# One sum of weights per pair moved from VectorE to an accumulating DMA, and a plain filler in the first pair of each chain, in a Mamba-2 layer in fp32

## The chip, the cores and the metric

The kernel runs on one core of a Trainium2 chip. The time is the device time of one execution in microseconds (us). TensorE (PE) multiplies, VectorE (DVE) and ScalarE (ACT) do the elementwise work, SyncE (SP) issues most transfers, and GpSimd (POOL) issues those that add to their destination.

## The reference, cut to what matters

DEPTH is 1, so the layer is the Mamba-2 mixer alone: 512 tokens, 2048 features, inner width 4096, 64 heads of 64 in 8 groups, a state of 128.

```python
def reference(x, ln_g, final_g, ssm_w_in, ...):
    hn = rmsnorm(x, ln_g[0])
    x = x + ssm_mixer(hn, ...)
    return rmsnorm(x, final_g)

def ssm_mixer(h, w_in, conv_w, conv_b, dt_bias, a_log, d_skip, norm_g, w_out):
    proj = h @ w_in                       # 2048 -> z 4096, x 4096, B 1024, C 1024, dt 64
    xbc = silu(causal_depthwise_conv(xbc, conv_w, conv_b))
    dt = softplus(dt + dt_bias)
    a = -exp(a_log)
    y = ssd_chunked_scan(xs * dt[..., None], dt * a, bm, cm)
    y = y + d_skip * xs
    y = rmsnorm(y * silu(z), norm_g)
    return y @ w_out                      # 4096 -> 2048
```

All is float32.

## The kernel before

**Products in three parts.** A float32 product is made of three matmuls on rounded halves: weights are split into `hi` (ACT rounds, L87) and `lo` (DVE subtracts, L88), the input into `xh` and `xl`, and PE adds hi times xh, hi times xl and lo times xh. So each 512 KB piece of weights costs one load, one cast on ACT and one subtraction on DVE before PE can use it. The halves of a piece lie in one of three `hi`/`lo` buffers; some pieces have buffers of their own (`h1h`/`h1l` for R11, `oh`/`ol` in the output projection).

**Plain tiles and pairs.** The input projection has 80 tiles of 128 columns. The first eight (`plain`: B0, C0, x0, z0, x1, z1, B1, C1) are computed directly, 16 k-steps of six 256-column matmuls each (`mm_k`). The other 72 go in 36 pairs (`quads`), one pair being two tiles, by a scheme of Strassen's kind: the two tiles times the two halves of the inner dimension make four blocks of weights R11, R12, R21, R22, and seven products replace eight. Each product (`product`) is 4 steps of six matmuls, and a pair is 28 steps (`QS`). The blocks used are R11, T1 = R11 + R12, T2 = T1 + R22, T4 = T2 + R21, R22, R21 and T3 = R12 + R22. T1 and T3 are made by a DMA that adds to the raw weights in SBUF (`q_fetch`, on POOL); T2 and T4 by an addition on DVE (`q_add`, L604). All of R11, T1, T2 and T4 live one after the other in one raw buffer (`ra`, three of them); R22 and R21 come in `rc` (two), R12 and T3 in `rb` (one). Sums of the input (`x_forms`, `x_form3`) are made once; `x_form3` overwrites a half of `xh` and `xl` and uses `xr`, the buffer of the convolution, as scratch.

**Steps and events.** PE's program is written as steps. `ev` maps a step to a list of events (loads, splits, sums, parts of the scan) that are written into the program when PE's stream reaches that step (`run`). Events of one step are written in the order in which they were added. PE, SP and POOL execute in exactly this order (`MANUAL`); the order of ACT and DVE is chosen when the kernel is built, by priority and by a model of the machine, and is then fixed. `urgent()` raises a priority. `q_events` gives the events of a pair relative to its first step b: R11's load at b-38, its split and the fetch for T1 at b-23, and so on.

**Order of the products.** A pair runs R11, T1, then the last product (T4) of the pair before it (`prev`), then T2, R22, R21, T3; its own T4 product becomes `prev` of the next pair. The first pair of a chain has no `prev`: it runs T1, R11, four steps with no matmuls, R22, T2, R21, T3. Two products that add to the same PSUM tile (T2 and T3 on `s_`, T1 and R22 on `r_`) have a read by DVE or ACT between them.

**The scan.** Each of 32 units (two heads) has its events at offsets from the first step of its x tile: `u_load` (decay sums to `csb`), `u_decay` (twelve ACT calls and a DVE multiply), `u_xt` (transposes), `u_state`, `u_yd` (the part inside a chunk), `u_yo` (the part from the state; its end stores y in `yscr` through SP). The kernel works in chunks of 128 tokens with one state at the middle. In a unit `u_state` and `u_yd` share a step, state first. Units 0 and 1 have offsets of their own (`ramp`).

**Output projection.** Six blocks: a list of plain pieces, a chain of four pairs, a list, a second chain, a list, and the last pieces. A plain piece is loaded and split by `get_out` and multiplied by `mm_o` for four token tiles t, two steps each. `opair` is the pair of this stage; its products are subtracted from `acc` by DVE (L889, L902, L907) and copied by ACT (L884, L916). `y_fetch` and `y_forms` prepare sums of y for a chain, `residual` adds x, `last_piece` prepares the last weights.

Of the kernel before, what the change touches and what calls it, by code (L numbers as in the profile page):

```python
# [1 line left out]

# [32 lines left out]
def mamba_layer(ctx: ExitStack, tc: tile.TileContext, d: dict, out: bass.AP):  # L35
# [80 lines left out]
    quads = seq[NPL // 2:]  # L116
    tile_of = {"z": 0, "x": 32, "B": 64, "C": 72}
    QS = 28
    at = {s: i * KT for i, s in enumerate(plain)}
    for i, pair in enumerate(quads):  # L120
        for s in pair:
            at[s] = NPL * KT + i * QS
    END = NPL * KT + len(quads) * QS
# [17 lines left out]
    for i, blk in enumerate(blocks):  # L141
        late = 4 if i == 0 or type(blocks[i - 1]) is tuple else 0
        base.append(base[-1] + (4 * QS if type(blk) is tuple else 8 * n_pieces(blk) + late))
# [16 lines left out]
    def get_out(n, name="ra"):  # L160
        if n < len(wo_order) and n not in opieces:
            opieces[n] = split_piece(load_piece(wo_src(*wo_order[n]), OSH, name), OSH,
                                     *((op, ("oh", "ol")) if n % 4 == 3 else (wp,)))
# [446 lines left out]
    def q_events(n, b, last, e=0, t1=0, lone=False):  # L610
        for o, f, a in ((-38 - e, q_load, ("R11", 0, 0, "ra")), (-23 - e, q_split, ("R11", True)),
                        (-23 - e, q_fetch, ("T1", "R11", 0, 1)), (-3 - e // 2 - t1, q_split, ("T1",)),
                        (-12 - e // 2, q_load, ("R22", 1, 1, "rc")), (1 - e // 2, q_add, ("T2", "T1", "R22")),
                        *(((5, q_split, ("R22",)), (9, q_split, ("T2",))) if lone else
                          ((5, q_split, ("T2",)), (9, q_split, ("R22",)))),
                        (-8, q_load, ("R21", 1, 0, "rc")), (12, q_add, ("T4", "T2", "R21")),
# [22 lines left out]
    def pair(n, prev):  # L639

        b = NPL * KT + n * QS
# [7 lines left out]
        def first(step):  # L649
            product(s_, W("R11"), 11, True, step)  # L650
            with urgent():
                S.copy(out=A[:, lo_], in_=s_)

        def second(step):
            product(r_, W("T1"), 1, True, step)
            with urgent():
                S.copy(out=sn[:, 1, :], in_=r_)

        if prev:
            first(b)  # L660
            second(b + 4)
            prev(b + 8)
        else:
            second(b)
            first(b + 4)
            for i in range(8, 12):
                run(b + i)
        def third(step):
            product(r_, W("R22"), 4, False, step)

        def fourth(step):
            product(s_, W("T2"), 2, False, step)
            with urgent():
                S.copy(out=sn[:, 0, :], in_=s_)

        for f, step in zip((fourth, third) if prev else (third, fourth), (b + 12, b + 16)):
            f(step)
# [28 lines left out]

    for g in range(1, G):
# [3 lines left out]
    ramp = [[66, 71, 63, 75, 87, 92], [56, 65, 50, 68, 86, 92]]  # L711
    for u in range(NU):
        w = ramp[u] if u < len(ramp) else [28, 42, 56, 65, 65, 71]
        for o, f in zip(w, (u_load, u_decay, u_xt, u_state, u_yd, u_yo)):
            add(at["x", u] + o, f, u)
    for n in range(len(quads)):
        q_events(n, NPL * KT + n * QS, n == len(quads) - 1, 0 if n else 14, lone=not n)
# [71 lines left out]
    for n in range(2, NPL):  # L789
        ps = None  # L790
        for k in range(KT):
# [11 lines left out]
        else:  # L803
            finish(n, ps)
    prev = None
# [65 lines left out]
    def opair(i, s, b, prev):  # L871
# [9 lines left out]
        def first(step):  # L881
            oproduct(s_, i, W("R11"), 11, True, step)
            with urgent():
                S.copy(out=A0, in_=s_)  # L884

        def second(step):
            oproduct(r_, i, W("T1"), 1, True, step)
            with urgent():
                V.tensor_tensor(out=q1, in0=q1, in1=r_, op=ALU.subtract)  # L889

        if prev:
            first(b)
            second(b + 4)
            prev(b + 8)
        else:
            second(b)
            first(b + 4)
            for k in range(8, 12):
                run(b + k)
        def third(step):  # L900
            oproduct(r_, i, W("R22"), 4, False, step)
            V.tensor_tensor(out=q0, in0=q0, in1=r_, op=ALU.subtract)  # L902

        def fourth(step):
            oproduct(s_, i, W("T2"), 2, False, step)
            with urgent():
                V.tensor_tensor(out=q0, in0=q0, in1=s_, op=ALU.subtract)  # L907

        for f, at_ in zip((fourth, third) if prev else (third, fourth), (b + 12, b + 16)):
            f(at_)  # L910
# [52 lines left out]
    for i, blk in enumerate(blocks):  # L963
        if type(blk) is tuple:
            for s in range(4):
                q_events(len(quads) + 4 * m + s, base[i] + s * QS, s == 3, 0, 3 if s == 0 else 0, s == 0)
# [34 lines left out]
    for kb, blk in enumerate(blocks[:-1]):  # L1001
        if type(blk) is tuple:
# [5 lines left out]
            continue  # L1008
        end = n0 + n_pieces(blk) + (n_pieces(blocks[kb + 1]) if kb + 2 < len(blocks) else 0)
        for s, pairs in blk:  # L1010
            ps = [None] * NC
            for p in pairs:
# [99 lines left out]
```

## Time and profile before

| | |
|---|---|
| three runs | 1297.31, 1289.81, 1293.4 us; median 1293.4 |
| profiled execution | 1295.7 us, of which the span from the first to the last instruction 1294.0 |
| granted clock of PE, mean | 0.991 |
| HBM read and written | 211.52 MB, 12.78 MB |

The profile's page cuts the span into 40 equal slices; a digit is the busy share of a slice in tenths, PEclk the clock that PE was granted, in tenths of full speed, DMA the mean busy share of the 16 DMA engines.

```profile
PE   8989899999999999999999999999999899999997
PEld 8989899999999999999999999999988899899885
DVE  5796988988989898998889899889857877887865
ACT  7667667677666757767685867778666445434433
POOL 0000001010000101010100001000000000000000
PEclk9989999999999999999999999999999999999999
DMA  9546657585676667667667677766637576647612
```

A slice is 32.35 us: the plain tiles fill the first four, the 36 pairs with the scan the next 25, the output projection the rest. The page also gives the chain of work that ended last, as shares of the span by engine.

```profile
PE 74%; DVE 11%; DMA 7%; issue 4%; ACT 3%; SPq 0%; POOL 0%; DVEq 0%; ACTq 0%; POOLq 0%
```

Of transfers, the page lists issues by what they load: count, size, and the median us from issue to landing.

```profile
rc<-in_wi SPq DMA_DIRECT2D x76, 512.0 KB, 5.9
...
ra<-in_wi POOLq DMA_DIRECT2D x36, 512.0 KB, 6.3
rb<-in_wi POOLq DMA_DIRECT2D x36, 512.0 KB, 5.9
csb<-cscr SPq DMA_DIRECT2D x32, 512.0 KB, 8.0
```

In all that follows a timeline row gives start (us), duration (us), engine, line, operation, what it writes and reads, shapes, the count, and in brackets how long the engine had been idle and what released it. A row of waits gives who waited for whom: us in total, times, longest.

### The profile page before, as it was taken

How to read it: one execution, taken by the hardware profiler on the slowest of the kernel's cores; microseconds unless marked ns; L12 is line 12 of the kernel's file. 1: busy time of each engine (PE TensorE's matmuls, PEld its weight loads, DVE VectorE, ACT ScalarE, POOL GpSimd, SP SyncE). 2: the span in 40 equal slices, each digit the busy share in tenths (PEclk: the TensorE clock that was granted, in tenths of full speed). 3: DMA queues.
4: the chain of work that ended last, by engine and by line, in shares of the span. 5: the costliest groups of instructions: out<-in, count | busy, mean ns of one | idle time of the engine just before them, and what ended most of it. 6: DMA issues, size and time to landing. Idle time of an engine off the chain costs nothing.

```text
span 1294.0 us, 24519 instructions
## 1 busy us (share of the span) xinstructions
PE 1252.1 (97%) x9932; PEld 1192.9 (92%) x9932; DVE 1084.3 (84%) x1449; ACT 826.6 (64%) x1357; POOL 77.5 (6%) x99
## 2 busy tenths in 40 slices
PE   8989899999999999999999999999999899999997
PEld 8989899999999999999999999999988899899885
DVE  5796988988989898998889899889857877887865
ACT  7667667677666757767685867778666445434433
POOL 0000001010000101010100001000000000000000
PEclk9989999999999999999999999999999999999999
DMA  9546657585676667667667677766637576647612
GB/s 356 179 141 172 162 161 174 143 215 142 192 197 174 159 169 183 164 176 199 162 161 195 151 188 171 212 155 154 185 105 258 146 199 199 197 119 229 183 57 98
DMA packets 70194, 225.90 MB, mean 175 GB/s; under 512 B 8384, under 2 KB 12800, under 8 KB 69952
## 3 DMA queue, kind: packets, MB, share of 16 engines
q1 hardware_dynamic: 56688, 176.34, 40.2%
q0 software_dynamic: 12672, 46.14, 22.1%
q8 instruction: 78, 1.28, 0.4%
q10 hardware_dynamic: 720, 1.84, 0.4%
q14 instruction: 36, 0.29, 0.1%
HBM read 211.52 MB, written 12.78 MB: 173 GB/s over the span
## 4 chain that ended last, share of the span: by engine, by line
PE 74%; DVE 11%; DMA 7%; issue 4%; ACT 3%; SPq 0%; POOL 0%; DVEq 0%; ACTq 0%; POOLq 0%
PE S L637 7%; PE S L635 7%; PE S L636 7%; PE mm L635 5%; PE mm L636 4%; PE R L635 4%; PE mm L637 4%; PE R L636 4%; PE R L637 4%; DVE lo L88 3%; PE mm L929 3%; PE mm L931 3%; PE mm L930 3%; PE yd L502 2%; PE mm L867 2%
## 5 line engine op out<-in xcount | busy, mean ns | idle before, releaser
L87 ACT CAST hi<-ra 128x1024 fp32r<-128x1024 f32 x150 | 154.7, 1046 | 159.5 <-DVE ra L604 72.9
L88 DVE TENSOR_TENSOR lo<-ra,hi 128x1024 fp32r<-128x1024 f32 x150 | 181.3, 1221 | 24.2 <-ACT hi L87 24.1
L635 PE MATMUL mm<-xh,hi 128*128 128x256 f32 x576 | 163.6, 284 | 0.0
L637 PE MATMUL mm<-xh,lo 128*128 128x256 f32 x576 | 160.6, 279 | 0.6 <-DVE lo L88 0.6
L636 PE MATMUL mm<-xl,hi 128*128 128x256 f32 x576 | 160.4, 278 | 0.0
L637 PE MATMUL R<-s,lo 128*128 128x256 f32 x576 | 160.3, 278 | 0.1
L635 PE MATMUL R<-s,hi 128*128 128x256 f32 x576 | 160.2, 278 | 0.0
L636 PE MATMUL R<-s,hi 128*128 128x256 f32 x576 | 160.2, 278 | 0.0
L88 DVE TENSOR_TENSOR lo<-rc,hi 128x1024 fp32r<-128x1024 f32 x94 | 114.9, 1223 | 28.5 <-ACT hi L87 28.1
L87 ACT CAST hi<-rc 128x1024 fp32r<-128x1024 f32 x94 | 98.4, 1047 | 50.8 <-issue 29.1
L604 DVE TENSOR_TENSOR ra<-ra,rc 128x1024 f32<-128x1024 f32 x88 | 107.7, 1224 | 13.3 <-DMA rc<-in_wi 11.8
L635 PEld LDWEIGHTS mm<-xh,hi 128*128 128x128 f32 x576 | 108.1, 188 | 5.2 <-issue 5.0
L637 PEld LDWEIGHTS mm<-xh,lo 128*128 128x128 f32 x576 | 109.2, 190 | 0.8 <-DVE lo L88 0.8
L637 PEld LDWEIGHTS R<-s,lo 128*128 128x128 f32 x576 | 109.1, 189 | 0.3 <-DVE lo L88 0.3
L635 PEld LDWEIGHTS R<-s,hi 128*128 128x128 f32 x576 | 108.2, 188 | 0.0
L636 PEld LDWEIGHTS mm<-xl,hi 128*128 128x128 f32 x576 | 108.2, 188 | 0.0
L636 PEld LDWEIGHTS R<-s,hi 128*128 128x128 f32 x576 | 108.1, 188 | 0.0
L637 PE MATMUL S<-xh,lo 128*128 128x256 f32 x288 | 83.5, 290 | 5.6 <-DVE lo L88 5.6
L635 PE MATMUL S<-xh,h1h 128*128 128x256 f32 x288 | 83.4, 290 | 1.0 <-DVE xr L398 1.0
L635 PE MATMUL S<-xh,hi 128*128 128x256 f32 x288 | 81.3, 282 | 2.2 <-ACT xh L577 1.3
L636 PE MATMUL S<-xl,hi 128*128 128x256 f32 x288 | 81.2, 282 | 0.7 <-DVE xl L578 0.7
L636 PE MATMUL S<-xl,h1h 128*128 128x256 f32 x288 | 80.8, 280 | 0.0
(452 smaller groups left out, 3940.8 us busy)
## 6 DMA issues: line engine op xcount, KB each, us to landing
rc<-in_wi SPq DMA_DIRECT2D x76, 512.0 KB, 5.9
ra<-in_wi SPq DMA_DIRECT2D x42, 512.0 KB, 6.2
rb<-in_wi SPq DMA_DIRECT2D x40, 512.0 KB, 6.9
ra<-in_wi POOLq DMA_DIRECT2D x36, 512.0 KB, 6.3
rb<-in_wi POOLq DMA_DIRECT2D x36, 512.0 KB, 5.9
csb<-cscr SPq DMA_DIRECT2D x32, 512.0 KB, 8.0
ra<-in_wo SPq DMA_DIRECT2D x26, 512.0 KB, 5.4
yscr<-xs SPq DMA_DIRECT2D x32, 256.0 KB, 2.6
```

Of the source, the lines that this page charges most:

```text
L87: S.copy(out=hi, in_=raw)
L88: V.tensor_tensor(out=lo, in0=raw, in1=hi, op=ALU.subtract)
L502: T.matmul(pyd[r, i, :], x[:, 2 * i, hh, :], m[:, i, hh::4, :], start=i == 0, stop=False, skip_group_check=True)
L604: V.tensor_tensor(out=raw, in0=raw, in1=qs[n][other], op=ALU.add)
L635: T.matmul(ps, hi[:, k, :], ah, start=first and k == 0, stop=False, skip_group_check=True)
L636: T.matmul(ps, hi[:, k, :], al, start=False, stop=False, skip_group_check=True)
L637: T.matmul(ps, lo[:, k, :], ah, start=False, stop=k == KH - 1, skip_group_check=True)
L867: T.matmul(ps[:, t, :], yh[:, k, tt], hi[:, k, :], start=st, stop=False, skip_group_check=True)
L929: T.matmul(ps, yh, hi, start=first and k == 0, stop=False)
L930: T.matmul(ps, yh, lo, start=False, stop=False)
L931: T.matmul(ps, yl, hi, start=False, stop=last and k == 1)
```

## The change

1. T4 is no longer added by DVE from T2 and the loaded R21. A third accumulating DMA (`q_fetch`) reads R21 again from HBM and adds it to T2's raw buffer, at b+10 instead of b+12. R21 is still loaded for its own product.
2. Four k-steps of the last plain tile (C1) are taken from the end of its loop and run as `prev` of pair 0, which now has the order of all other pairs, so that the pairs begin at step 124 instead of 128 (`QB`). In each output chain the last two token tiles of the plain piece ahead of it (`bridge`, `tail`) do the same. The special order of first pairs, `lone` and `t1` go. Every step from the pairs on has a lower number; no matmul is added or removed.
3. The scan's events are added by kind: all loads, decays and transposes, then `u_yd`, then `g_bt` and `g_cb`, then `u_state` and `u_yo`. In a unit's shared step yd runs first and state last.
4. The plain output pieces with buffers of their own are now numbers 4, 8, 12, 16, 20 instead of 3, 7, 11, 15, 19, 23, and `y_fetch` and `y_forms` move by a few steps.

```diff
+    QB = NPL * KT - 4
...
-            at[s] = NPL * KT + i * QS
-    END = NPL * KT + len(quads) * QS
+            at[s] = QB + i * QS
+    END = QB + len(quads) * QS
...
         late = 4 if i == 0 or type(blocks[i - 1]) is tuple else 0
+        late -= 4 if type(blocks[min(i + 1, len(blocks) - 1)]) is tuple else 0
...
-                                     *((op, ("oh", "ol")) if n % 4 == 3 else (wp,)))
+                                     *((op, ("oh", "ol")) if n and n % 4 == 0 else (wp,)))
...
-    def q_events(n, b, last, e=0, t1=0, lone=False):
+    def q_events(n, b, last, e=0):
         for o, f, a in ((-38 - e, q_load, ("R11", 0, 0, "ra")), (-23 - e, q_split, ("R11", True)),
-                        (-23 - e, q_fetch, ("T1", "R11", 0, 1)), (-3 - e // 2 - t1, q_split, ("T1",)),
+                        (-23 - e, q_fetch, ("T1", "R11", 0, 1)), (-3 - e // 2, q_split, ("T1",)),
                         (-12 - e // 2, q_load, ("R22", 1, 1, "rc")), (1 - e // 2, q_add, ("T2", "T1", "R22")),
-                        *(((5, q_split, ("R22",)), (9, q_split, ("T2",))) if lone else
-                          ((5, q_split, ("T2",)), (9, q_split, ("R22",)))),
-                        (-8, q_load, ("R21", 1, 0, "rc")), (12, q_add, ("T4", "T2", "R21")),
+                        (5, q_split, ("T2",)), (9, q_split, ("R22",)),
+                        (-8, q_load, ("R21", 1, 0, "rc")), (10, q_fetch, ("T4", "T2", 1, 0)),
                         (13, q_split, ("R21",)),
                         (-7, q_load, ("R12", 0, 1, "rb")), (-7, q_fetch, ("T3", "R12", 1, 1)),
                         (17, q_split, ("T3",)), (23 if last else 29, q_split, ("T4",))):
...
-        if prev:
-            first(b)
-            second(b + 4)
-            prev(b + 8)
-        else:
-            second(b)
-            first(b + 4)
-            for i in range(8, 12):
-                run(b + i)
...
-        for f, step in zip((fourth, third) if prev else (third, fourth), (b + 12, b + 16)):
-            f(step)
...
+        product(s_, W("R11"), 11, True, b)
+        with urgent():
+            S.copy(out=A[:, lo_], in_=s_)
+        product(r_, W("T1"), 1, True, b + 4)
+        with urgent():
+            S.copy(out=sn[:, 1, :], in_=r_)
+        prev(b + 8)
+        product(s_, W("T2"), 2, False, b + 12)
+        with urgent():
+            S.copy(out=sn[:, 0, :], in_=s_)
+        product(r_, W("R22"), 4, False, b + 16)
...
+    def add_units(*kinds):
+        for u in range(NU):
+            for i, f in kinds:
+                add(at["x", u] + steps[u][i], f, u)
+
+    add_units((0, u_load), (1, u_decay), (2, u_xt))
+    add_units((4, u_yd))
     for g in range(1, G):
         add(at["B", g] + (30 if ("B", g) in plain else 93), g_bt, g)
         for i in range(2):
             add(at["x", 4 * g] + 28, g_cb, g, i)
...
-        for o, f in zip(w, (u_load, u_decay, u_xt, u_state, u_yd, u_yo)):
-            add(at["x", u] + o, f, u)
+    add_units((3, u_state), (5, u_yo))
...
-        for k in range(KT):
+        for k in range(KT if n < NPL - 1 else KT - 4):
...
-    prev = None
+
+    def prev(step):
+        for i in range(4):
+            run(step + i)
+            mm_k(ps, pieces[2 * NPL - 1], 4 + i, KT - 4 + i)
+        finish(NPL - 1, ps)
...
+        oproduct(s_, i, W("R11"), 11, True, b)
+        with urgent():
+            S.copy(out=A0, in_=s_)
+        oproduct(r_, i, W("T1"), 1, True, b + 4)
+        with urgent():
+            V.tensor_tensor(out=q1, in0=q1, in1=r_, op=ALU.subtract)
+        prev(b + 8)
+        oproduct(s_, i, W("T2"), 2, False, b + 12)
+        with urgent():
+            V.tensor_tensor(out=q0, in0=q0, in1=s_, op=ALU.subtract)
+        oproduct(r_, i, W("R22"), 4, False, b + 16)
+        V.tensor_tensor(out=q0, in0=q0, in1=r_, op=ALU.subtract)
...
-                add(base[i] - ((50, 32), (54, 32))[m][j], y_fetch, m, j)
-                add(base[i] - ((39, 24), (47, 24))[m][j], y_forms, m, j)
+                add(base[i] - ((48, 30), (54, 32))[m][j], y_fetch, m, j)
+                add(base[i] - ((36, 23), (47, 24))[m][j], y_forms, m, j)
...
+        def tail(ps, w, y, t, s, first, step):
+            for k in range(2):
+                run(step + k)
+            mm_o(ps, w, y, t, first, True)
+            a = acc[:, t, s * L:(s + 1) * L]
+            with urgent():
+                V.tensor_tensor(out=a, in0=ps, in1=a, op=ALU.add)
...
+                    if type(blocks[kb + 1]) is tuple and s == 3 and n0 + 1 == n_end and t > 1:
+                        bridge.append(partial(tail, ps[t], opieces[n0], ys[p], t, s, p == pairs[0]))
+                        continue
...
+        if bridge:
+            def prev(step, parts=bridge):
+                for i, f in enumerate(parts):
+                    f(step + 2 * i)
```

More of the change, by code (lines that the diff above doesn't have):

```diff
@@ L1 @@
 from contextlib import ExitStack
+from functools import partial
 import numpy as np
@@ L639, in pair @@
     def pair(n, prev):
-        b = NPL * KT + n * QS
+        b = QB + n * QS
         (kp, ip), (kq, iq) = quads[n]
@@ L647, in pair @@
         A = ps_mm.tile([P, L], F32, name="mm")
[L649 to L657, printed above, removed]
-        if prev:
-            first(b)
-            second(b + 4)
-            prev(b + 8)
-        else:
-            second(b)
-            first(b + 4)
-            for i in range(8, 12):
-                run(b + i)
[L668 to L674, printed above, removed]
-        for f, step in zip((fourth, third) if prev else (third, fourth), (b + 12, b + 16)):
-            f(step)
+        product(s_, W("R11"), 11, True, b)
[9 more added lines that the diff above has]
+        product(r_, W("R22"), 4, False, b + 16)
         with urgent():
@@ L705, in add @@
         ev.setdefault(step, []).append((f, a))
+    ramp = [[66, 71, 63, 75, 87, 92], [56, 65, 50, 68, 86, 92]]
+    steps = [ramp[u] if u < len(ramp) else [28, 42, 56, 65, 65, 71] for u in range(NU)]
+    def add_units(*kinds):
[4 more added lines that the diff above has]
+    add_units((4, u_yd))
     for g in range(1, G):
@@ L710, in mamba_layer @@
             add(at["x", 4 * g] + 28, g_cb, g, i)
-    ramp = [[66, 71, 63, 75, 87, 92], [56, 65, 50, 68, 86, 92]]
-    for u in range(NU):
-        w = ramp[u] if u < len(ramp) else [28, 42, 56, 65, 65, 71]
-        for o, f in zip(w, (u_load, u_decay, u_xt, u_state, u_yd, u_yo)):
-            add(at["x", u] + o, f, u)
+    add_units((3, u_state), (5, u_yo))
     for n in range(len(quads)):
-        q_events(n, NPL * KT + n * QS, n == len(quads) - 1, 0 if n else 14, lone=not n)
+        q_events(n, QB + n * QS, n == len(quads) - 1, 0 if n else 14)
     for i in range(4):
@@ L802, in mamba_layer @@
             st["x0"] = ps
-        else:
+        elif n < NPL - 1:
             finish(n, ps)
-    prev = None
+    def prev(step):
[3 more added lines that the diff above has]
+        finish(NPL - 1, ps)
     for n in range(len(quads)):
@@ L879, in opair @@
         A0 = ps_mm.tile([P, 2, LH], F32, name="mm")
[L881 to L910, printed above, removed]
+        oproduct(s_, i, W("R11"), 11, True, b)
[10 more added lines that the diff above has]
+        V.tensor_tensor(out=q0, in0=q0, in1=r_, op=ALU.subtract)
         oproduct(A0, i, W("R21"), 12, False, b + 20)
@@ L965, in mamba_layer @@
             for s in range(4):
-                q_events(len(quads) + 4 * m + s, base[i] + s * QS, s == 3, 0, 3 if s == 0 else 0, s == 0)
+                q_events(len(quads) + 4 * m + s, base[i] + s * QS, s == 3)
             for j in range(2):
-                add(base[i] - ((50, 32), (54, 32))[m][j], y_fetch, m, j)
-                add(base[i] - ((39, 24), (47, 24))[m][j], y_forms, m, j)
+                add(base[i] - ((48, 30), (54, 32))[m][j], y_fetch, m, j)
+                add(base[i] - ((36, 23), (47, 24))[m][j], y_forms, m, j)
             m += 1
@@ L1008, in mamba_layer @@
             continue
+        def tail(ps, w, y, t, s, first, step):
[5 more added lines that the diff above has]
+                V.tensor_tensor(out=a, in0=ps, in1=a, op=ALU.add)
+        bridge = []
+        n_end = n0 + n_pieces(blk)
         end = n0 + n_pieces(blk) + (n_pieces(blocks[kb + 1]) if kb + 2 < len(blocks) else 0)
```

## The prediction

> **What bounds the kernel now.** I read the stretches first: the busy time of each engine in six stretches that follow the kernel's stages. Columns: stretch, its length, then busy us (and instructions) of PE, weight loads, DVE, ACT, POOL; granted clock, DMA share, GB/s.
>
> ```profile
> 0.00:120.00 120.00, 108.25 (x853) 105.30 (x853) 86.37 (x143) 81.81 (x128) 3.38 (x13) 0.97 0.64 221
> 120.00:172.00 52.00, 46.65 (x367) 44.68 (x366) 46.92 (x62) 35.15 (x62) 3.69 (x5) 0.93 0.62 158
> 172.00:1005.00 833.00, 827.64 (x6893) 795.60 (x6892) 729.92 (x948) 588.36 (x1005) 57.52 (x67) 1.00 0.66 175
> 1005.00:1136.00 131.00, 126.19 (x870) 117.23 (x870) 106.16 (x131) 58.01 (x73) 7.70 (x9) 0.99 0.63 180
> 1136.00:1212.00 76.00, 73.75 (x643) 73.18 (x643) 59.99 (x67) 34.70 (x40) 5.18 (x6) 1.00 0.67 187
> 1212.00:1294.00 82.00, 69.66 (x317) 56.89 (x315) 54.97 (x103) 28.61 (x52) 0.00 (x0) 0.97 0.27 97
> sum 1294.00, PE 1252.15 PEld 1192.89 DVE 1084.34 ACT 826.64 POOL 77.48; mean PE 208.69 PEld 198.81 DVE 180.72 ACT 137.77 POOL 12.91
> ```
>
> PE is busy for 1252.15 of 1294.00 us. The change takes no matmul away, so all that it can win is PE's lost time: the idle part of a stretch, and (1 - clock) times its length. I leave out 0 to 120 (ahead of the first pair) and the output's end. The first pairs (120 to 172) lose 52.00 - 46.65 = 5.35 us idle and 0.07 x 52 = 3.64 by the clock: 9.0. The long run of pairs loses 833.00 - 827.64 = 5.4, at clock 1.00. The first output chain (1005 to 1136) loses 4.8 + 0.01 x 131 = 6.1, the second 2.25, and the end 2.9 (two waits below). Together **25.6 us: the cap on any gain**.
>
> Then the waits of PE, first in 120 to 172, then from 927 on; columns: total, times, longest.
>
> ```profile
> PE S L635 <- ACT xh L577: 1.3, 1, 1.3
> PE S L635 <- DVE xr L398: 1.0, 1, 1.0
> PE S L635 <- ACT hi L87: 0.9, 1, 0.9
> PE S L637 <- DVE lo L88: 0.8, 1, 0.8
> PE S L636 <- DVE xl L578: 0.7, 1, 0.7
> PE mm L637 <- DVE lo L88: 0.6, 1, 0.6
> ```
>
> ```profile
> PE mm L867 <- DVE acc L907: 2.5, 1, 2.5
> PE mm L869 <- DVE lo L88: 1.8, 2, 1.4
> PE mm L867 <- ACT mm L916: 1.7, 1, 1.7
> PE mm L867 <- DVE acc L889: 1.7, 1, 1.7
> PE mm L930 <- DVE lo L88: 1.2, 1, 1.2
> ```
>
> So PE starves in a handful of places at the starts of the three chains, nearly always for DVE or for ACT behind it.
>
> **Part 1: T4 = T2 + R21 by DMA instead of DVE.**
>
> ```profile
> L604 DVE TENSOR_TENSOR ra<-ra,rc 128x1024 f32<-128x1024 f32 x88 | 107.7, 1224 | 13.3 <-DMA rc<-in_wi 11.8
> ```
>
> Half of the 88 adds go: 44 x 1.224 = 53.9 us of DVE. In their place come 44 accumulating transfers of 512 KB on POOL.
>
> ```profile
> q0 software_dynamic: 12672, 46.14, 22.1%
> L598 POOL DMA_DIRECT2D ra<-in_wi x36: 844/847/999, 95.2 to 892.2; - x36
> DMA to landing us min/median/max: 5.3/6.0/8.4
> ```
>
> The 88 of today hold the 16 engines for 22.1% of 1294 us, 3.25 us each; in the long run 36 x 3.25 us in 833 add 0.14 to the share of 0.66. POOL gains 44 x 0.85 = 37 us on 77, HBM reads 23 MB (R21 is still loaded for its own product).
>
> Does the freed DVE time reach PE? In the long run of pairs it does not. The longest wait of PE there, and DVE's rows ahead of it:
>
> ```profile
> 501.43 0.39 PE L637 MATMUL S<-xh,lo 128*128 128x256 f32 x1 [1.54 <-DVE lo L88]
> ```
>
> ```profile
> 487.52 1.22 DVE L604 TENSOR_TENSOR ra<-ra,rc 128x1024 f32<-128x1024 f32 x1
> 488.67 1.22 DVE L88 TENSOR_TENSOR h1l<-ra,h1h 128x1024 fp32r<-128x1024 f32 x1
> 492.59 1.23 DVE L88 TENSOR_TENSOR lo<-rc,hi 128x1024 fp32r<-128x1024 f32 x1 [2.71 <-ACT hi L87]
> ```
>
> The T4 add at 487.52 stands ahead of a 2.71 us idle in which DVE waits for ACT; without it DVE only idles longer, and the backlog that delays PE begins after 492.59. I take **0** for this stretch; its bounds are -5.4 (all of its loss) and +2 (the build orders DVE and ACT anew, and a cast falls behind another).
>
> At the first pair it does reach PE:
>
> ```profile
> 131.98 1.23 DVE L604 TENSOR_TENSOR ra<-ra,rc 128x1024 f32<-128x1024 f32 x1
> 133.11 1.23 DVE L88 TENSOR_TENSOR lo<-rc,hi 128x1024 fp32r<-128x1024 f32 x1
> ```
>
> The add stands right ahead of R21's lo part, for which PE waits 0.6: **-0.6**.
>
> **Part 2: the first pair of a chain gets the order of the others.** R11's product now comes first and 24 plain matmuls fill the gap, so T1's sum for the next pair starts sooner (R11's one buffer, h1, comes free eight steps sooner against the same matmuls). A step, six matmuls, is 0.68 us, as the last step of one T1 product shows with the start of a T4 product; eight steps are 5.4.
>
> ```profile
> 509.27 0.28 PE L635 MATMUL R<-s,hi 128*128 128x256 f32 x1
> 509.95 0.28 PE L635 MATMUL mm<-xh,hi 128*128 128x256 f32 x1
> ```
>
> Today that sum comes too late:
>
> ```profile
> 137.36 1.05 ACT L87 CAST hi<-ra 128x1024 fp32r<-128x1024 f32 x1 [3.42 <-DMA ra<-in_wi]
> 138.45 1.23 DVE L88 TENSOR_TENSOR lo<-ra,hi 128x1024 fp32r<-128x1024 f32 x1 [1.43 <-ACT hi L87]
> ```
>
> DVE stands 1.43 us for it, with the last x_form3 queued behind, for which PE waits 1.3 + 0.7 at T3's product. Those 1.43 and the 1.23 of the add cover the 2.0: **-2.0**. The 1.0 for L398 I keep: C1's tail now ends eight steps later, but DVE reaches its read earlier; bounds -1.0 to +3.
>
> A new wait: the last plain piece keeps its hi/lo buffer (three in all) until the tail ends at b+12, and R22's cast needs it. R22's product starts at b+16, 4 x 0.68 = 2.7 us later; cast and lo take 1.05 + 1.23 = 2.28, which leaves 0.4 on a full DVE. Queued behind a waiting cast on ACT are the next casts, and behind those DVE. I take **+1.0** (0 to 2.3).
>
> The decay factors of unit 2: SP issues in written order.
>
> ```profile
> 149.02 0.33 SPq L524 DMA_DIRECT2D yscr<-xs  x1
> 149.39 0.43 SPq L440 DMA_DIRECT2D csb<-cscr  x1
> ```
>
> Today csb's load stands behind the store of unit 1's y, which waits for DVE. After the change the load has step 152 and the store 156, so it goes some 4 steps (2.7 us) sooner, ACT's twelve decay calls too, and the cast for which pair 1's T3 waits 0.9 + 0.8 comes in time: **-1.7** (0 to -1.7). R22's and R11's loads stay behind that store.
>
> Of the clock's 3.64 I let go the share of the stalls that go, 4.3 of 5.3: **-2.9** (0 to -3.64). The Trainium skill ("TensorE: Matmul & The Clock Gate", Part 1) says that the array falls to half rate after an idle window of about 3.4 us. Here the clock is 0.93 in a stretch whose longest wait is 1.3, so short stalls close together do it too; by the rule alone these 2.9 would not be there and the forecast would be 1284. The row decides.
>
> First pairs together: -0.6 - 2.0 + 1.0 - 1.7 - 2.9 = **-6.2**.
>
> **Part 3: the output chains.** Today's first pair runs T1, R11, R22, T2, R21, T3 without a filler. PE waits 2.5 at T3 for L907, 1.7 at R22 for L889.
>
> ```profile
> 1021.68 1.99 ACT L87 CAST hi<-ra 128x1024 fp32r<-128x1024 f32 x2 [4.95 <-DMA ra<-in_wq]
> ```
>
> ```profile
> 1022.76 1.23 DVE L88 TENSOR_TENSOR lo<-ra,hi 128x1024 fp32r<-128x1024 f32 x1 [2.06 <-ACT hi L87]
> 1023.90 0.68 DVE L907 TENSOR_TENSOR acc<-acc,mm 128x512 f32<-128x512 f32 x1
> ```
>
> L907 stands on DVE behind a cast that waits for the next pair's T1 sum. In the new order T2 and T3 are eight steps apart instead of four, T1 and R22 too, which is 2.7 us more for each read, and T1's sum starts sooner: **-2.5 and -1.7**, and the clock's **-1.3** with them. T2 is wanted 2.7 us sooner than now against the matmuls before it, and y_forms moves one to three steps ahead; its wait (1.4 of the 1.8) stays and I add **+0.5** (0 to 2). The other 0.4 of the 1.8 stands behind a T4 add: **-0.4**. The 1.2 for L930 is the first piece after the second chain, whose buffer becomes a separate one; half goes: **-0.6** (0 to -1.2). L916 keeps its 1.7. Sum: **-6.0**.
>
> **Part 4: yd ahead of state** swaps two sets of matmuls in a unit and removes none. State's result is wanted six steps (4.1 us) after, and only its two small urgent conversions lie between; SP's loads, grouped ahead within a step, pass no store but the one of Part 2. I take 0 (to +1).
>
> **Sum:** -6.2 + 0 - 6.0 + 0 = -12.2 us. The profiled execution took 1295.7 (span 1294.0 and 1.7 around it), so its like would take 1283.5; the median of the three runs is 1293.4, and I predict from it: **1281**.
>
> **Rivals.** *The gain stays on DVE.* ACT and DVE get a new order from the build, and the waits that I ascribe to DVE go over to ACT or the transfers. For it: the long run above, where DVE has idle time and PE waits all the same. Against it: L907 and L889 go by PE's own order. Then only 2.5 + 1.7 + 0.6 + 1.2 go and 1 to 3 come back: about 3 us, 1290.
>
> *The third transfer lands late,* which ends slower. POOL issues in order: T4's fetch comes after the next pair's T1 fetch.
>
> ```profile
> 490.29 0.86 POOL L598 DMA_DIRECT2D ra<-in_wi  x1 [1.45 <-DVE h1l L88]
> 501.10 1.03 ACT L87 CAST hi<-ra 128x1024 fp32r<-128x1024 f32 x1
> ```
>
> It could go at 491.15. T4's cast stands at 501.10 today, 9.95 us later; the slowest landing so far took 8.4, and if it queues behind all of T1's 3.25 it takes 11.65: ACT then stands 1.7 us, with the next cast behind it. PE is hit when the sum lands later than 507.7 (T4's product at 509.95 less 2.28), which is 16.5 us after the issue. From there each us late costs 44 us over 44 pairs; half a us is 22: 1303 on top of the forecast's gains, 1315 without them. Against it: engines that are free a third of the time, and a median landing of 6.0 us. The Trainium skill ("SBUF — State Buffer", SBUF: two separate sides) speaks for this rival: a transfer issued from GpSimd gets no descriptors while certain DVE operations hold the port that both share, so each of the three fetches could stand. The rows do not show it: 844 to 999 ns per issue with DVE 84% busy. It would need 8 us more per landing, and I leave the rival its small chance.
>
> **How the numbers follow.** Forecast, 1274 to 1286: 0.58. Still better, with the long run's 5.4 and the kept waits gone too: 0.06. Gain stays on DVE, within 6.5 us of 1293.4: 0.23. Late transfer, 1300 and more: 0.13. A measurement of this kernel tells 0.5%, 6.5 us, from no change. So faster 0.64, same 0.23, slower 0.13. The range, **1272 to 1297**, leaves out the late transfer and the ends of the others; the cap would be 1293.4 - 25.6 = 1267.8.
>
> **What would show it.** Right: DVE busy near 1030, POOL near 115, 132 software transfers with 69 MB, DMA share near 0.80 in the long run; no wait of PE for L907 and L889; clock near 0.98 in the first pairs; the waits for lo in the long run about as now. Wrong: idle time of ACT that ends with a landing of ra at T4's cast in every pair; a wait for R22 of 2 us in the first pair; PE waiting for L398 longer than 1.0; landings of software transfers above 9 us.

## The result, and the profile after

| | before | after |
|---|---|---|
| median | 1295.1 us | 1323.8 us |
| runs | 1289.8 to 1297.3 | 1320.7 to 1327.9 |
| profiled execution, span | 1294.0 us | 1319.4 us |

Each median is of four runs. The ratio is 1.024, with a 95% interval of 1.0203 to 1.0277: slower by 29 us, where 1281 (1272 to 1297) was predicted. The stretches of the kernel after, cut at its own stages (columns as in the prediction):

```profile
118.00:174.00 56.00, 48.86 (x383) 46.67 (x382) 46.48 (x61) 37.20 (x67) 5.23 (x6) 0.94 0.65 166
174.00:1024.00 850.00, 828.35 (x6869) 791.91 (x6868) 694.44 (x912) 588.91 (x1005) 88.89 (x102) 0.99 0.76 192
...
sum 1319.40, PE 1257.52 PEld 1193.11 DVE 1041.91 ACT 829.03 POOL 116.82; mean PE 209.59 PEld 198.85 DVE 173.65 ACT 138.17 POOL 19.47
```

DVE did lose its 42 us (1084.34 to 1041.91), and PE's work is the same within 5.4 us. But the long run and the list behind it went from 833 to 850 us, and PE's idle part in it from 5.4 to 850.00 - 828.35 = 21.7. Less work on DVE did not shorten that stretch. The waits of PE, first in the long run (174 to 947), then from 1000 to the end; columns: total, times, longest:

```profile
PE S L639 <- DVE lo L89: 12.5, 14, 1.9
```

```profile
PE mm L863 <- ACT mm L894: 7.2, 4, 4.1
PE mm L907 <- ACT hi L88: 3.7, 1, 3.7
PE mm L863 <- ACT hi L88: 2.6, 2, 1.9
```

(L88 and L89 are now the split, L601 the fetch, L607 T2's addition, L637 to L639 a product of a pair, L863 to L865 one of an output pair, L907 to L909 a plain output piece, L894 the copy of an output pair's sum.) The waits for the accumulations L889 and L907 of before are gone, as predicted, and larger ones stand in their place. The long run waited 4.8 us for `lo` before. The page's rows of T2's addition and of the transfers:

```profile
q0 software_dynamic: 19008, 69.21, 30.9%
...
L607 DVE TENSOR_TENSOR ra<-ra,rc 128x1024 f32<-128x1024 f32 x44 | 53.9, 1224 | 39.7 <-DMA rc<-in_wi 39.4
...
ra<-in_wi POOLq DMA_DIRECT2D x72, 512.0 KB, 9.0
```

DVE, with less to do, now stands 39.4 us ahead of T2's addition for R22's load (11.8 for twice as many additions before). That row, and the median landing of 9.0 us (6.3 before), are where the experiments begin.

### The profile page after: what moved, and what is told of

It reads as the page before. It is cut to its first block, busy times and chain, and to the rows that moved or that the text cites. A ratio compares the mean times of both kernels' runs of the same rounds, so it can differ in the third digit from the quotient of the medians.

```text
span 1319.4 us, 24643 instructions
## 1 busy us (share of the span) xinstructions
PE 1257.5 (95%) x9932; PEld 1193.1 (90%) x9932; DVE 1041.9 (79%) x1405; ACT 829.0 (63%) x1359; POOL 116.8 (9%) x143
## 4 chain that ended last, share of the span: by engine, by line
PE 67%; DVE 11%; ACT 10%; DMA 8%; issue 4%; SPq 0%; DVEq 0%; ACTq 0%
PE S L639 6%; PE S L637 5%; PE S L638 5%; PE mm L908 4%; PE mm L909 4%; PE mm L907 4%; PE mm L637 3%; PE R L637 3%; PE R L639 3%; PE R L638 3%; PE mm L638 3%; PE mm L639 3%; ACT hi L88 3%; DVE lo L89 3%; PE mm L863 3%
## 5 line engine op out<-in xcount | busy, mean ns | idle before, releaser
L88 ACT CAST hi<-ra 128x1024 fp32r<-128x1024 f32 x153 | 158.3, 1047 | 194.8 <-DVE ra L607 96.3
L89 DVE TENSOR_TENSOR lo<-ra,hi 128x1024 fp32r<-128x1024 f32 x153 | 186.6, 1220 | 28.3 <-ACT hi L88 27.7
L639 PE MATMUL R<-s,lo 128*128 128x256 f32 x576 | 160.9, 279 | 6.0 <-DVE lo L89 6.0
L637 PE MATMUL mm<-xh,hi 128*128 128x256 f32 x576 | 162.3, 282 | 0.4 <-ACT mm L668 0.4
L637 PE MATMUL R<-s,hi 128*128 128x256 f32 x576 | 160.8, 279 | 0.7 <-ACT hi L88 0.7
L639 PE MATMUL mm<-xh,lo 128*128 128x256 f32 x576 | 159.8, 277 | 0.1
L89 DVE TENSOR_TENSOR lo<-rc,hi 128x1024 fp32r<-128x1024 f32 x92 | 112.5, 1223 | 36.8 <-ACT hi L88 36.3
L88 ACT CAST hi<-rc 128x1024 fp32r<-128x1024 f32 x92 | 95.9, 1045 | 37.1 <-issue 17.9
L639 PEld LDWEIGHTS R<-s,lo 128*128 128x128 f32 x576 | 109.3, 190 | 7.0 <-DVE lo L89 7.0
L637 PEld LDWEIGHTS R<-s,hi 128*128 128x128 f32 x576 | 109.0, 189 | 1.4 <-ACT hi L88 1.3
L639 PEld LDWEIGHTS mm<-xh,lo 128*128 128x128 f32 x576 | 108.6, 189 | 0.3 <-DVE lo L89 0.3
L637 PEld LDWEIGHTS mm<-xh,hi 128*128 128x128 f32 x576 | 108.3, 188 | 0.7 <-ACT mm L668 0.6
L639 PE MATMUL S<-xh,lo 128*128 128x256 f32 x288 | 85.7, 298 | 13.2 <-DVE lo L89 13.2
L601 POOL DMA_DIRECT2D rb<-in_wi x36 | 31.0, 861 | 676.5 <-DMA rb<-in_wi 379.7
L607 DVE TENSOR_TENSOR ra<-ra,rc 128x1024 f32<-128x1024 f32 x44 | 53.9, 1224 | 39.7 <-DMA rc<-in_wi 39.4
L637 PE MATMUL S<-xh,hi 128*128 128x256 f32 x288 | 82.5, 287 | 1.7 <-ACT hi L88 1.7
L637 PE MATMUL S<-xh,h1h 128*128 128x256 f32 x288 | 82.5, 287 | 0.0
```

The costliest lines, as they stand in the source:

```text
L88: S.copy(out=hi, in_=raw)
L89: V.tensor_tensor(out=lo, in0=raw, in1=hi, op=ALU.subtract)
L601: nc.gpsimd.dma_start(raw, q_src(n, half, tile_)[0], accum_op=ALU.add)
L607: V.tensor_tensor(out=raw, in0=raw, in1=qs[n][other], op=ALU.add)
L637: T.matmul(ps, hi[:, k, :], ah, start=first and k == 0, stop=False, skip_group_check=True)
L639: T.matmul(ps, lo[:, k, :], ah, start=False, stop=k == KH - 1, skip_group_check=True)
```

## The experiments

One table holds what all runs gave. The first columns are medians and ratios against the kernel before on the same chip. The others are worked out from one profiled execution of each kernel by the starts of matmuls, so a difference of 2 or 3 us in one column can be that execution's own (e4's ran 3.6 us under its median): the first two pairs; the six *uncovered* pairs; the other 27 pairs of numbers 2 to 34; and each output chain with the list ahead of it. Each cut holds the same number of matmuls in every kernel. An uncovered pair is the second after a B/C pair (numbers 6, 11, 16, 21, 26, 31): yd, state and yo of a unit run 65 to 71 steps after its x tile began, that is two pairs later, and a B/C pair has no unit. So these six pairs have no scan matmuls between their products, and last 20 to 21 us instead of 22 to 24.

| run | us | ratio, 95% | first two | six uncovered | other 27 | list+chain 1 | list+chain 2 |
|---|---|---|---|---|---|---|---|
| before | 1295.1 | | 54.6 | 124.5 | 612.2 | 161.6 | 127.2 |
| after | 1323.8 | 1.0240 (1.0203-1.0277) | 56.8 | 137.9 | 610.4 | 169.3 | 130.2 |
| e1 T4 by DMA alone | 1307.3 | 1.0088 (1.0065-1.0111) | 57.6 | 128.1 | 613.2 | 158.7 | 135.0 |
| e2 chain starts alone | 1294.3 | 1.0003 (0.9990-1.0015) | 51.6 | 125.2 | 614.0 | 163.4 | 128.5 |
| e3 scan order alone | 1306.0 | 1.0087 (1.0072-1.0102) | 51.0 | 140.5 | 609.5 | 161.1 | 127.8 |
| e4 all but T4 by DMA | 1309.2 | 1.0112 (1.0090-1.0134) | 51.8 | 136.0 | 611.1 | 161.0 | 126.9 |
| e5 e3, R22 loaded sooner | 1286.0 | 0.9936 (0.9913-0.9958) | 52.6 | 121.7 | 608.7 | 158.7 | 128.1 |
| e6 yd and state swapped alone | 1309.6 | 1.0133 (1.0114-1.0152) | 52.6 | 141.1 | 612.4 | 159.0 | 130.8 |
| e7 e1, T4's fetch first | 1300.9 | 1.0064 (1.0049-1.0079) | 58.2 | 128.5 | 612.7 | 155.0 | 129.6 |
| e8 e2, second read of y later | 1289.9 | 0.9974 (0.9962-0.9986) | 51.7 | 124.0 | 613.1 | 157.7 | 126.6 |
| e9 e4 with both repairs | 1282.9 | 0.9919 (0.9887-0.9950) | 51.3 | 118.4 | 609.0 | 158.8 | 128.8 |
| e10 e9 with T4 by DMA, first | 1298.4 | 1.0043 (1.0024-1.0062) | 54.2 | 127.8 | 609.5 | 162.7 | 127.8 |
| e11 before, R22 loaded sooner | 1290.9 | 0.9973 (0.9954-0.9992) | 53.5 | 120.9 | 613.1 | 160.9 | 129.0 |
| e12 before, an idle transfer | 1299.0 | 1.0046 (1.0025-1.0068) | 53.8 | 129.8 | 613.0 | 160.2 | 130.8 |
| e13 e9, an idle transfer | 1285.7 | 0.9942 (0.9908-0.9977) | 53.3 | 119.6 | 608.4 | 155.7 | 130.1 |
| e14 before, two idle transfers | 1302.9 | 1.0065 (1.0042-1.0087) | 54.3 | 124.7 | 612.2 | 160.2 | 136.0 |

The 27 covered pairs stay within 608 to 614 us whatever was done. Time is won and lost in the first two pairs, the six and the chains.

### The change in parts: e1 to e4

e1 is the kernel before with one edit:

```diff
-(12, q_add, ("T4", "T2", "R21")),
+(10, q_fetch, ("T4", "T2", 1, 0)),
```

> Before, with T4 made by the third accumulating DMA and nothing else. Theory A (the third transfer costs: it makes loads land later, so DVE and ACT start late): most of the 28 us of the change are here, 1308 to 1318, PE's waits in the long run of pairs near 18 us instead of 5, landings of the ra transfers from POOL near 9 us. Theory B (the new start of the chains costs): 1290 to 1298. Theory C (the order of the scan costs): 1290 to 1298.

e2 has the new chain starts and output pieces (edits 2 and 4 of the change), with T4 on DVE and the scan's old order.

> Before, with the new start of the three chains (filler, bridge, steps, buffers of the plain output pieces) alone; T4 stays on DVE, the scan's order stays. Theory A: 1285 to 1298, the long run loses about 5 us as before. Theory B: 1305 to 1315, with a wait of 2 to 3 us for R22 in the first pair and waits of 3 to 4 us at the output chains. Theory C: 1285 to 1298.

e3 has the scan's new order alone (edit 3).

> Before, with the scan's events in the new order (yd first, state last, loads first) alone. Theories A and B: within 4 us of before, 1289 to 1298. Theory C: 1302 to 1312, with more waits for lo in the long run.

e4 is the change with T4's addition on DVE again.

> The changed kernel with T4 added by DVE again. Theory A: back to 1285 to 1300. Theory B or C: 1310 to 1320, the same waits as in the changed kernel.

Two of the three parts lose: T4 by DMA 12.8 us, the scan's order 11.5 us; the chain starts, from which nearly all of the 12 us of gain were to come, gave nothing. The three add to 24 of the 29 us. e3 came as theory C had it and e1 just under theory A (with PE's waits in the long run at 8.4 us, not 18), so no one theory holds the whole, and each part was followed by itself. e4, just under the range of B and C, says the same: with T4 back on DVE the change still loses 15 us, and T4's transfer costs 14.6 in it. Between e4 and the kernel after, the six uncovered pairs differ by only 1.9 us, the first two by 5.0 and the two lists with chains by 11.6. Of the 39.4 us that DVE stood for R22 in the long run, e4 still has 26.2, and e1 has 14.9.

### The scan's order: e5, e6, e11

All of e3's loss is in the six uncovered pairs: 140.5 against 124.5. Pair 16 begins at 483.2 us in the one kernel and at 483.1 in the other, so rows can be compared as they stand. The timeline of the kernel before, ACT, SP and DVE:

```profile
468.47 0.27 ACT L403 CAST stsh<-yo 128x128 fp32r<-128x128 f32 x1
476.73 0.68 DVE L523 TENSOR_TENSOR xs<-xs,z 128x512 f32<-128x512 f32 x1
477.44 0.33 SPq L524 DMA_DIRECT2D yscr<-xs  x1
477.87 0.37 SPq L81 DMA_DIRECT2D rc<-in_wi  x1
482.93 1.23 DVE L604 TENSOR_TENSOR ra<-ra,rc 128x1024 f32<-128x1024 f32 x1 [1.65 <-DMA rc<-in_wi]
```

And e3's:

```profile
470.05 0.27 ACT L403 CAST stsh<-yo 128x128 fp32r<-128x128 f32 x1 [1.52 <-PE yo L488]
477.74 0.69 DVE L523 TENSOR_TENSOR xs<-xs,z 128x512 f32<-128x512 f32 x1
478.45 0.33 SPq L524 DMA_DIRECT2D yscr<-xs  x1
478.88 0.37 SPq L81 DMA_DIRECT2D rc<-in_wi  x1
485.11 1.23 DVE L604 TENSOR_TENSOR ra<-ra,rc 128x1024 f32<-128x1024 f32 x1 [2.26 <-DMA rc<-in_wi]
```

State behind yd is converted 1.58 us later (ACT now waits for PE), y is finished 1.01 us later (L523, its last operation), and its store on SP goes 1.01 us later. SP issues in written order, and R22's load for the next pair (step b-12) is written right behind that store (step b-13). It leaves 1.01 us later, T2's addition starts 2.18 later (the load also took longer to land), and T2's casts and the rest of the pair's follow. A covered pair has scan matmuls for PE meanwhile, and the 27 of them lost nothing (609.5 against 612.2); in an uncovered one PE stands. e5 takes e3 and moves only that load ahead of the store; e11 moves it in the kernel before; e6 makes only the swap in that kernel (second diff; the steps of units 0 and 1 go with their events), without grouping the others.

```diff
-(-12 - e // 2, q_load, ("R22", 1, 1, "rc"))
+(-14 if 0 < n < len(quads) else -12 - e // 2, q_load, ("R22", 1, 1, "rc"))
```

```diff
-        for o, f in zip(w, (u_load, u_decay, u_xt, u_state, u_yd, u_yo)):
+        for o, f in zip(w, (u_load, u_decay, u_xt, u_yd, u_state, u_yo)):
```

> The kernel before with the scan's new order alone (which took 1306) and, besides, R22's load of each scan pair at b-14 instead of b-12, so that SyncE issues it ahead of the store of y at b-13. Theory S (state last makes y late; the store of y holds SyncE, R22's load behind it starts 1.0 to 1.4 us later, T2's sum is late in every fifth pair, which has no scan matmuls to cover it): the fifth pairs go back to 20 to 21 us and the time to 1291 to 1297. Rival O (the build's other order of VectorE and ScalarE costs the time, whatever the load does): 1303 to 1308, with the fifth pairs at 22 to 25 us as before.

> The kernel before with one thing changed: in each unit yd's events stand ahead of state's, unit by unit as before; loads, g_bt and g_cb keep their places in the order. If yd ahead of state is what costs (theory S): 1303 to 1308, and the store of y is about 1 us later against the pair behind it. If it is the grouping of loads, decays and transposes of all units ahead of the rest: 1292 to 1297.

> The kernel before with R22's load at b-14 and nothing else. If the load's place behind the store of y already costs in the old scan order, this gains what the fifth pairs lose there, 1 to 1.5 us each in five of six: 1286 to 1291. If the gain of 8 needs the new scan order: 1291 to 1295.

All three go the way of theory S. e6 shows that the swap is the cause: 1309.6, above the 1303 to 1308 of S, with 141.1 in its uncovered pairs and y's store 0.9 us later against pair 16. e5 is 20 us faster than e3, and 8 us faster than the kernel before, below the range that S gave it. e5's rows for pair 16, which begins at 478.1 there:

```profile
467.25 0.33 SPq L81 DMA_DIRECT2D rc<-in_wi  x1
472.33 0.33 SPq L524 DMA_DIRECT2D yscr<-xs  x1
476.20 1.23 DVE L604 TENSOR_TENSOR ra<-ra,rc 128x1024 f32<-128x1024 f32 x1
```

R22's load is 10.8 us ahead of the pair instead of 4.2 (e3), and DVE adds without standing for it. The main row of PE's waits in the long run, first e3's, then e5's:

```profile
PE S L637 <- DVE lo L88: 12.0, 12, 1.9
```

```profile
PE S L637 <- DVE lo L88: 3.8, 9, 1.1
```

e11 shows that the load stood badly in the kernel before, too (3 us). e5 gains 5 us more than e11, so the new order of the scan seems worth something once its late store blocks nothing: its other 27 pairs take 608.7 against 613.1. What in that order gives these was not tried.

### The chain starts: e8

e2 wins 3.0 us in the first two pairs (granted clock 0.97 there, 0.94 before) and gives it back. In the list ahead of the first chain PE stands 3.8 us for a piece of weights. The row of PE's waits in e2, and SP's timeline there:

```profile
PE mm L901 <- ACT hi L88: 3.8, 1, 3.8
```

```profile
979.23 0.33 SPq L82 DMA_DIRECT2D ra<-in_wo  x1
990.81 1.49 SPq L809 DMA_DIRECT2D yr<-yscr  x2
992.35 0.42 SPq L82 DMA_DIRECT2D ra<-in_wo  x1
```

SP in the kernel before:

```profile
982.05 0.33 SPq L81 DMA_DIRECT2D ra<-in_wo  x1
992.30 1.49 SPq L819 DMA_DIRECT2D yr<-yscr  x2
```

The second read of y for the chain (`y_fetch`, j = 1) must wait for its buffer until 991. With 12 matmuls of the list moved into the chain, the plain pieces came to stand four steps later against the chain's steps, while this read moved by two: it now stands ahead of the last piece's load and holds it for 11 us. e8 is e2 with one number changed:

```diff
-                add(base[i] - ((48, 30), (54, 32))[m][j], y_fetch, m, j)
+                add(base[i] - ((48, 28), (54, 32))[m][j], y_fetch, m, j)
```

> The first pairs' part of the change alone (which took 1294) with one number changed: the second read of y for the first output chain at 28 steps ahead of the chain instead of 30, so that SyncE issues the load of the list's last piece of weights ahead of it instead of behind it. If that piece's late load is what takes back the gain (PE waits 3.9 us for its cast, and 2.1 at T2 behind it): the list before the first chain is 5 us shorter and the time 1286 to 1291. If the gain is lost elsewhere: 1293 to 1296.

The load now leaves with the piece before it, ahead of the read:

```profile
978.46 2.79 SPq L82 DMA_DIRECT2D ra<-in_wo  x2
990.03 1.49 SPq L809 DMA_DIRECT2D yr<-yscr  x2
```

The list and first chain take 157.7 us instead of 163.4, and the kernel 1289.9: the chain starts are worth 4 us once this is mended.

### T4 by DMA: e7, e12, e10, e13, e14

In the kernel after, T1's fetch of the next pair and T4's leave POOL together:

```profile
607.67 1.73 POOL L601 DMA_DIRECT2D ra<-in_wi  x2 [1.47 <-DVE h1l L89]
```

e7 asks whether T4's place behind T1 is the price, e12 whether the bytes are: it leaves T4 on DVE and adds, behind that addition, a 512 KB copy from the weights to a place in HBM that nobody reads.

```diff
-                        *(((5, q_split, ("R22",)), (9, q_split, ("T2",))) if lone else
-                          ((5, q_split, ("T2",)), (9, q_split, ("R22",)))),
-                        (-8, q_load, ("R21", 1, 0, "rc")), (12, q_add, ("T4", "T2", "R21")),
+                        *(((5, q_split, ("R22",)), (9, q_split, ("T2",)), (9, q_fetch, ("T4", "T2", 1, 0))) if lone else
+                          ((5, q_split, ("T2",)), (5, q_fetch, ("T4", "T2", 1, 0)), (9, q_split, ("R22",)))),
+                        (-8, q_load, ("R21", 1, 0, "rc")), 
```

```diff
-        qs[n][f] = raw
+        qs[n][f] = raw; (f == "T4") and nc.gpsimd.dma_start(spare[n][:, 0:q_src(n, 1, 0)[1][1], 0:q_src(n, 1, 0)[1][2]], q_src(n, 1, 0)[0])
```

(`spare` holds one such place per pair; its declaration is left out here.)

> The kernel before with T4 by a third accumulating transfer (which took 1307 when that transfer stood at b+10), now issued right behind T2's split at b+5, ahead of the next pair's T1 transfer instead of behind it. Theory Q (T4's transfer queues behind T1's of the next pair, 0.5 us after it, and lands in 9 to 13 us): the landing falls to 6 to 8 us, T4's casts stop waiting, and the time is 1292 to 1298. Rival D (the 23 MB more that the DMA engines move delay all loads near them, in whatever order): 1304 to 1309. A third way: T1's sum is now the one that lands late, then the next pair's T1 waits and it is over 1308.

> The kernel before, T4 still added by VectorE, and right behind that addition one more transfer of the same 512 KB on GpSimd's queue, from the weights to a spare place in HBM that nobody reads: 44 of them, 23 MB, with nothing waiting for one; the orders of VectorE, ScalarE and SyncE are as before. It leaves no work out. Rival D (the bytes and the queue are the price: the loads and the T1 and T3 sums near it land later): 1300 to 1308. Theory W (only the wait of T4's cast for its own transfer is the price): 1293 to 1297.

e7 fell between its theories: 7 us above before, and below e1 by 6 us in the medians but 3 in the ratios, whose intervals overlap. The landings did not get shorter (median 7.4 us, in e1 6.7, before 6.0). In the profiled executions the gain is all in the output chains (155.0 + 129.6 against 158.7 + 135.0), where PE's waits for the copy L916 (of an output pair's sum, on ACT) fell from 6.2 us to 0.8; which edit of the order does that was not settled. e12 came out just below the range of theory D: 5 us for transfers that no instruction waits for. T1's and T3's own landings kept a median of 6.1; what moved were loads, and DVE stood 18.6 us for R22 in the long run (11.8 before). 5.3 of e12's loss is in the uncovered pairs, 4.3 of it in one of them (number 6). By the Trainium skill ("Trainium Kernel Development and Optimization", Key Constraints) the transfers issued from SP, ACT and POOL run on the same 16 DMA engines and interleave; this run fits that, with R22's and R21's loads from SP landing in 6.2 us at the median (5.9 before). The software queue's share says how long one copy holds the 16 engines: (26.5% x 1299.8 - 22.1% x 1294.0) / 44 = 1.33 us; an accumulating one holds them 3.25.

e9 is e4 with the edits of e5 and e8; e10 is the whole change with these two and with T4's fetch in e7's place.

> The change without the third transfer (T4 by VectorE again; it took 1309), with R22's load at b-14 in the scan pairs and the second read of y for the first output chain at 28 steps ahead of it. If the two losses are what the two single edits showed (-8 against the kernel before by the first with the new scan order, -4 by the second with the new first pairs), they add: 1279 to 1284. If the gains cover the same idle time: 1285 to 1289. If the new order of a chain start and of the scan together cost something of their own: 1294 and more.

> The whole change with three repairs: R22's load at b-14, the second read of y at 28 steps, and T4's transfer right behind T2's split. If the third transfer keeps the price that it had alone in this place (+6 to +7 on the kernel before): 1285 to 1291, that is 6 to 7 above the same kernel without it. If its price comes only with the late loads that the other repairs mend: 1279 to 1284. If it grows on the tighter schedule: over 1292.

The two repairs add as expected: e9 takes **1282.9 us**, 0.8% (0.5 to 1.1) below the kernel before, and is the best of all. T4's transfer then costs 15 us on it (e10), more than alone, as the last of its three cases had it; 9.4 of them are in the six uncovered pairs. The timeline of e10 in the long run, POOL and ACT, then the rows of waits of ACT and DVE over that run:

```profile
377.34 2.01 POOL L601 DMA_DIRECT2D ra<-in_wi  x2
390.20 1.05 ACT L88 CAST hi<-ra 128x1024 fp32r<-128x1024 f32 x1 [3.51 <-DMA ra<-in_wi]
```

```profile
ACT hi L88 <- DMA ra<-in_wi: 25.9, 13, 4.5
...
DVE lo L89 <- ACT hi L88: 61.5, 50, 4.2
```

Of the two transfers issued between 377.3 and 379.4 one lands shortly before 390.2, 11 to 13 us on. ACT stands 3.51 for it with the next casts behind; over the run ACT stands 25.9 us so, where e9 has no such row, and DVE behind ACT 61.5 us against e9's 17.3:

```profile
DVE lo L89 <- ACT hi L88: 17.3, 21, 2.0
```

How much of the 15 are bytes, and how much that wait? e13 is e9 with e12's idle transfer, e14 the kernel before with two of them.

> The version without the third transfer and with both repairs (it took 1283), T4 by VectorE, plus one idle transfer of 512 KB per pair behind T4's addition, as in the earlier run on the kernel before (where it cost 5). With T4 by the third transfer the same schedule took 1298. If the bytes are most of those 15 us: 1293 to 1298. If the wait of ScalarE for a landing is most of them, since nobody waits for the idle one: 1283 to 1289.

> The kernel before with two idle transfers of 512 KB per pair instead of one: by the queue's share one held the 16 engines for 1.33 us, two hold them for 2.7, near the 3.25 of an accumulating one. If the cost goes with the engines' time: 1302 to 1307, nearly what T4's transfer alone cost (1307). If one idle transfer's 5 us are what any extra work on the queue gives: 1297 to 1301.

e13 takes 1285.7: one copy per pair costs 3 us there (the two intervals overlap), with no wait of ACT for a landing. But it holds the engines 1.33 us, not 3.25. Scaled by that, an estimate, the bytes would be about 7 of the 15 and the wait the other half; with two copies e9 was not run. e14 costs 8 us, two thirds of e1's 12.8, for 2.7 us of engines' time per pair (31.0% of 1301.5 in the queue): in the looser schedule of before the bytes look like the larger part. By what path they cost is not shown: e12 lost 5.3 us in the uncovered pairs, e14 0.2 there and 8.8 in the second list and chain, where PE's idle time rose from 5.3 to 11.5. In e1's long run ACT stands only 0.5 us for such a landing, but in its output chains eight times, for 30.0 us. The row of ACT's waits there, before and e1:

```profile
ACT hi L87 <- DMA ra<-in_wq: 8.8, 2, 4.9
```

```profile
ACT hi L87 <- DMA ra<-in_wq: 30.0, 8, 5.1
```

About half of the increase is idle time that ACT had anyway: it stood 44.0 us for PE's matmuls there before and 33.1 in e1. What PE loses in e1's second list and chain is 3.8 us more idle time (9.1 against 5.3) and a granted clock of 0.97 instead of 1.00. Over the output stage its row for the copy L916, 1.7 us before, is:

```profile
PE mm L867 <- ACT mm L916: 6.2, 4, 2.9
```

How much of all this goes back to T4's landings was not isolated: in e7 ACT stands 35.4 us for them in the same place, and PE waits only 0.8 for L916.

## Why the prediction was wrong

**What bounds the kernel.** The cap of 25.6 us on a gain stands: the best version won 11. But I read PE's waits as waits for DVE. Rows such as `PE S <- DVE lo` name the last link; behind `lo` stood a cast, behind the cast T2's sum, behind it R22's load, and behind that a store on SP. Taking work off DVE shortened nothing: neither column of the long run is shorter in e1.

**Part 1.** "I take **0** for this stretch; its bounds are -5.4 ... and +2": with T4's transfer alone the six uncovered pairs lost 3.6 us and the other 27 pairs 1.0, over the upper bound. The 0.6 of the first pair did not come either: the first two pairs took 57.6 us in e1 against 54.6, with 7.3 us of PE's waits there instead of 5.3 and a granted clock of 0.88 instead of 0.94. The rival "the third transfer lands late" named the right mechanism with a wrong point. It started to charge when PE itself was late, 16.5 us after the issue, and called for 8 us more per landing. But ACT stands as soon as the cast is next in its order (9.95 us, as that sum had it), and what stands behind the cast waits too, as in e10; landings of 11 to 13 us were enough. And it charged all 44 pairs alike, where in e1 the six lost 3.6 us, the first two 3.0 and the chains 4.9 together, and the other 27 next to nothing. That bytes alone cost 5 to 8 us (e12, e14) was in no rival: I had the DMA share at 0.80 (it is 0.76) and no price for it.

**Part 2.** The new order of the first pair did win: -3.0 in e2, not -6.2. The new wait for R22's buffer was taken as "+1.0 (0 to 2.3)" and is one of 2.9 us in the kernel after:

```profile
PE R L639 <- DVE lo L89: 3.7, 2, 2.9
```

That is over its bound, because I had counted the cast and the subtraction alone. R22's cast was done at 129.2, and its `lo` began at 131.37, behind a decay multiplication, R11's `lo` and an x_form3 on DVE:

```profile
127.36 1.75 DVE L464 TENSOR_TENSOR m<-m,cbm 128x1536 f32<-128x1536 f32 x1
...
131.37 1.22 DVE L89 TENSOR_TENSOR lo<-rc,hi 128x1024 fp32r<-128x1024 f32 x1
```

The clock's -2.9 did not come: the first pairs have 0.94 in the kernel after, by two short stretches of 3.4 us in which 0.50 was granted. The first, from 133.0, comes right behind the new wait, with PE busy for 0.48 of the 3.4 us ahead; the second is from 167.1.

**Part 3.** The waits for L907 and L889 went, as predicted. The step that failed was "y_forms moves one to three steps ahead", which I priced at +0.5: its read of y moved past the load of the list's last piece on SP, 3.8 us of PE there and 1.9 at T2 behind it. I had weighed the casts and subtractions of that step and not its transfer. Mended (e8), the two lists with chains win 157.7 + 126.6 against 161.6 + 127.2, 4.5 of the 6.0 us.

**Part 4** is the largest miss: "I take 0 (to +1)", and it costs 11.5 alone, 15.7 as a bare swap (e6). "State's result is wanted six steps (4.1 us) after" was true for PE. But I stopped at the product yo, and did not follow it to y's store and to what SP has written behind that store. I wrote that SP's loads pass no store but one; nothing passed anything, the store itself came later. And the range and the chances gave this no rival.

**The sum.** Of the signs listed, DVE near 1030 (1041.9), POOL near 115 (116.8), 132 transfers with 69 MB and the two vanished waits came; the DMA share (0.76), the clock near 0.98 in the first pairs (0.94) and the unchanged waits for lo in the long run (4.8 to 14.8) did not; of the contrary ones, landings above 9 us (13.0) and a wait for R22 above 2 us (2.9) came, and ACT's idle time for T4 in every pair did not (2.8 us in two waits in the long run). Forecast -12.2; measured +28.7, as e1's 12.8, e3's 11.5 and e2's -0.1 with 4.5 between them.

## What to carry to other kernels

Before work is taken off a busy engine, follow the wait of the bound engine back through every link, to a transfer and the queue that issues it: a load written behind a store that waits for late data is a wait of its own, and moving one load by two steps was worth 20 us here where that store had become late, and 3 in the kernel before. Price a delay at the place with the least cover (here six of 36 pairs), not over all places alike. An addition given to an accumulating transfer costs bytes that everybody's loads feel, and a landing that an in-order engine will stand for, with all that is queued behind the cast; no run here shows it paying.

## What the hardware showed

- Accumulating transfers issued close together land late. With two per pair they took 5.3 to 8.4 us (up to 9.8 in e9), with three up to 13.0. In the kernel after, the 64 that left within 2.5 us of the one before took 9.3 us at the median, the rest 5.9. A plain copy of as many bytes on the same queue holds the DMA engines 1.33 us, an accumulating one 3.25.
- The clock went by how much PE stood in a short stretch, not by the longest single wait. Cut narrowly, the trace of the kernel before has a granted clock of 0.51 and 0.50 in two stretches of 3.4 us in the first pairs, from 145.2 and from 165.7. PE was busy for 1.59 and 1.74 us of the 3.4 ahead of each, in several waits of which the longest was 1.3. In e9 the first pairs (119 to 171) ran at a granted clock of 1.00 (the row of that stretch), with these waits of PE:

```profile
119.00:171.00 52.00, 46.16 (x395) 44.67 (x394) 48.31 (x65) 37.70 (x67) 4.31 (x5) 1.00 0.61 163
```

```profile
PE R L639 <- DVE lo L89: 3.6, 2, 2.9
PE S L639 <- DVE lo L89: 1.6, 1, 1.6
```

The 2.9 lies from 131.7 to 134.6. Cut into 3.4 us at 129.7, 133.1 and 136.5, as the half-clock stretches of that trace fall, PE was still busy for 2.01 and 1.88 of each. By the Trainium skill's rule ("TensorE: Matmul & The Clock Gate", Part 1), an idle window of about 3.4 us, the clock would have stayed up in both kernels. That fits e9 and not before, and the trace decides. So the prediction's reading, that short stalls close together lower the clock, holds. Where the limit lies was not measured: in e2 PE was busy for 1.61 of 3.4 us from 830.4, and the clock stayed at 1.00.
